# Up-projection of a hybrid encoder step: the A22 T4 product of two sets by seven inner products, its operands streamed from DRAM

## The chip, the cores and the metric

The kernel runs on one core of a Trainium2 chip. The metric is the device time of one execution in microseconds. Three runs of the kernel before gave 1512.61, 1510.98 and 1512.71 us (median 1512.61).

## The reference, cut to what matters

One encoder layer on 1024 prompt and 32 sample tokens, all in fp32: an input projection with attention, short convolution and gates, an output projection, and then the MLP, in which the change lies:

```
x = x + merged @ w_o
f = jnp.square(jax.nn.relu(rmsnorm(x, g_ffn) @ w_up)) @ w_down    # w_up 1024 x 4096
x = x + f
```

The row factor of rmsnorm is applied after w_down (its square, `rs2`), so the up-projection needs only x times g_ffn.

## The kernel before, in words

Tokens lie along the free dimension: T = 1056 columns, halves of 528 (`TH`) and quarters of 264 (`TQ`). Every fp32 product is three matmuls of a high and a low part (`h`, `l`): the high part is a cast on ScalarE, the low part a subtraction on VectorE. One "set" is 256 columns of w_up, so there are 16 sets; a set is a 2 x 2 matrix of weight blocks (A11 to A22, with four k-blocks of 128 each) times a 2 x 2 matrix of token blocks (B11 to B22). It is done by the seven products of Strassen's scheme in Winograd's form: A11 B11, A12 B21, S1 T1, S2 T2, S3 T3, S4 B22 and A22 T4, where S1 to S4 are sums of weight blocks and T1 to T4 sums of token blocks. One such outer product has, for each of two quarters, 4 k-blocks x 3 matmuls of 264 columns = 12 matmuls (L362 to L376).

Sets 0 and 1 run alone. From set 2 on, sets run in pairs (`seven_pair`, L480), seven pairs in all. In a pair the products A12 B21 of both sets are one product of a 2 x 2 matrix of weight blocks by a 2 x 2 matrix of token blocks, and that one again is done by seven inner products of 2 k-blocks x 3 = 6 matmuls each (`inner_product`, L348): 42 matmuls instead of 48. Its token sums (`inner_t`) stay in SBUF. The other twelve products of a pair are outer ones.

`manual_schedule` fixes the order on TensorE, ScalarE, VectorE and POOL as it is written. `run` (L617) advances the pair's body by one step (to the next `yield`) and then every generator in `side` by one step, so `after(n, g)` does the first piece of g behind the body's step n + 1. DMAs issued on SP are placed by the compiler. Side work: `prepare` (L217) splits the outer weights of a set (POOL sums, ScalarE casts, VectorE low parts), `prepare_inner` (L256) those of the joined product, `pair_loads` fetches weights, `mid_sums` (L1731) makes and stores the T1 to T4 of the hidden values after relu and square, `mean_squares` (L1702) makes `rs2`. Split outer weights live in four buffers (`SHB`), raw weights in four, large tiles (4224 bytes a partition, `blk`) in 37. PSUM groups come from a pool of four (`many`) and one of two (`few`), two more tiles belong to `tps`. In the last pair the first weights and hidden tiles of the down-projection are split as well (L2416 to L2420), and the down-projection's loop (L2432) splits the next step's weights one step ahead.

Of the kernel before, what the change touches and what calls it, by code (L numbers as in the profile page):

```python
# [15 lines left out]
P = 128  # L16
# [59 lines left out]
def tile_step(  # L76
# [81 lines left out]
    def group(name, n=TT, pool_=None):  # L158
        p_ = pool_ or pools[turn[0] % len(pools)]
        turn[0] += pool_ is None  # L160
        return p_.tile([P, TW], F32, tag="g", name=name)[:, :n]
# [24 lines left out]
        nc.scalar.copy(d[:, 0, :], src)  # L186
        dve(d[:, 1, :], src, d[:, 0, :].bitcast(F32), op=sub)

    def half_w(src, name):
        h, l = (wpool[0].tile([P, 4, P], F32R, tag=f"s{x}", name=f"s{x}{name}", bufs=SHB) for x in "hl")  # L190
        nc.scalar.copy(h, src)  # L191
        return (h, l), partial(dve, l, src, h.bitcast(F32), op=sub)

# [62 lines left out]
    def prepare_inner(key, odd):  # L256
# [38 lines left out]
        low()  # L295
        yield

    def inner_operands(name, g, load):
# [48 lines left out]

    def inner_product(name, w, b, p_=None, pool_=None):  # L348

        o = {"B11": low_t[0][0], "B21": low_t[1][0], "B22": low_t[1][1]}.get(b) or inner_t[b]  # L350
        new = p_ is None
        if new:
            p_ = group(f"ps_in{name}", TQ, pool_)
        on = dict(skip_group_check=not new)
        wh, wl = w
        for k in range(2):
            nc.tensor.matmul(p_, wh[:, k, :], o[:, 0, k, :], start=new and k == 0, stop=False, **on)
            nc.tensor.matmul(p_, wh[:, k, :], o[:, 1, k, :], start=False, stop=False, **on)
            nc.tensor.matmul(p_, wl[:, k, :], o[:, 0, k, :], start=False, stop=k == 1, **on)
        return p_  # L360
# [116 lines left out]
                done("near")  # L477
        done("21")

    def seven_pair(s0, s1, key, m, last, after=({}, {})):  # L480

        def tile_of(k, i):
            return wpool[0].tile([P, TQ], F32, tag=k, name=f"{k}_{s0}{i}")
# [42 lines left out]
        def sixth(i, t):  # L526
            product(i, "A22", "T4", t, x[i][t])
            last(m(i, 1), q[t][1], x[i][t])

        for f in (first, second, third, fourth):  # L530
            for t in range(2):
                f(0, t)
                yield
# [51 lines left out]
    def after(n, *gens):  # L585
        for _ in range(n):
            yield
        for g in gens:
            yield from g
# [18 lines left out]
    def pair_side(nm, a, b, then=None):  # L608

        order = ("S1", "A11", "S2", "S3", "S4", "A22")  # L610
        side.append(after(3, prepare(f"{nm}{b}", (4, 6, 8, 10, 13, 15), (f"{nm}{a}e", f"{nm}{a}o", 1), order)))
# [179 lines left out]
    def md(k, s_):  # L791
# [8 lines left out]
    cvd = dpool.tile([4, 2, P, T], F32, name="cvd")  # L800
    ed = dpool.tile([KD, P, T], F32, name="ed")
    edt = dpool.tile([P, 2, 2 * P], F32, name="edt")
    inner_s = {
        (k, p): {a: dpool.tile([P, NP_, P], F32, name=f"di{k}{p}{a}") for a in ("S1", "S2", "S3", "S4")}
        for k in NESTED for p in range(2)
# [851 lines left out]
    def wo_unit(n):  # L1657
# [41 lines left out]

        return load, body  # L1700

    def mean_squares():  # L1702
# [12 lines left out]

# [28 lines left out]
        dve(tb[:, 0, :], m2[:, a], ta[:, 1, :], op=sub)  # L1744
        nc.sync.dma_start(md("T4", s_), tb[:, 0, :])

    def up_hooks(i, s_, m):
# [24 lines left out]

        def c21():
            side.append(later_(partial(done, 1, 0, "B21")))

        return {"11": c11, "22": c22, "12": c12, "near": near, "21": c21}

# [4 lines left out]
    def up_pair(a, b):  # L1782
        ms = {}

        def m(i, j):
            if (i, j) not in ms:
                ms[i, j] = blk(f"m{j + 1}_{(a, b)[i]}")
            return ms[i, j]

        return seven_pair(  # L1790
            f"u{a}", f"u{b}", f"u{a}y", m, relu2, [up_hooks(i, (a, b)[i], partial(m, i)) for i in range(2)]
        )

    def up_source(a, b):
# [592 lines left out]
    with tc.manual_schedule(engines=MM):  # L2387
        def all_t():
            o, e = x1[-1], x1[-2]
            raw_t[KD // 2 - 1] = sums(KD // 2 - 1, e, o)  # L2390
            yield
            for n, parts in enumerate(LATE_T):
                for k, j in parts:
                    part_raw(f"T{k}", j)
                if n == 2:
                    for j in range(3):
                        fetch_t(j, 1)
                yield

        side += [all_t(), first_w.pop(), after(2, prepare("u1", at=(9, 11, 13, 15, 17, 19)))]  # L2400
# [10 lines left out]
        run(up_set(1))  # L2411
        for a in range(2, NSET, 2):
            more = a + 2 < NSET
            pair_side("u", a, a + 1, up_source(a + 2, a + 3) if more else None)
            if not more:
                side.append(after(13, call(fetch_upto, 2), call(sum_w, 0), call(sum_w, 1)))  # L2416
                side.append(after(15, *(call(fetch_mid, "P1", 0, j) for j in range(4))))
                side.append(after(18, call(high_w, 0), call(high_mid, "P1", 0, 0), call(low_w, 0), call(low_mid, "P1", 0, 0)))
                side.append(after(20, *(call(f, "P1", 0, j) for j in (1, 2) for f in (high_mid, low_mid))))
                side.append(after(23, call(high_mid, "P1", 0, 3), call(low_mid, "P1", 0, 3), call(fetch_mid, "P1", 1, 0), call(fetch_mid, "P1", 1, 1)))  # L2420
            run(up_pair(a, a + 1))
        while side:
            run(range(1))
# [152 lines left out]
```

## Time and profile before

| what | value |
|---|---|
| median of three runs | 1512.61 us |
| profiled execution | 1510.11 us |
| its span, first to last instruction | 1508.4 us |
| granted TensorE clock, mean | 0.999 |
| TensorE busy | 1495.6 us |
| VectorE / ScalarE / POOL busy | 1149.1 / 794.6 / 377.7 us |

A busy TensorE only says that a matmul was under way: matmuls overlap, a duration of 0.28 us stands beside a spacing of 0.12 us between starts. Idle time of another engine costs nothing by itself.

### The profile page before, as it was taken

Reading aid. Unit: us, or ns where it says so; the run is one execution under the profiler, and the core shown is the slowest. Engines: PE = TensorE matmul, PEld = TensorE weight load, DVE = VectorE, ACT = ScalarE, POOL = GpSimd, SP = SyncE. Lnnn points to the kernel's source line nnn. Section 1 sums busy time; section 2 is a strip of 40 time slices with the busy share of each in tenths; the row PEclk is TensorE's granted clock in tenths of the full one; section 3 lists DMA queues with packets and bytes.
Section 4 is the critical chain, followed back from the end, with each engine's and each line's share of the span. In section 5 each row is a group of like instructions: output and inputs, shape, how many; then the busy total and the mean of one; then the engine's idle time right before and its main releaser. Section 6 shows DMA issues by size and latency. Waiting matters only on the chain.

```text
span 1508.4 us, 29451 instructions
## 1 busy us (share of the span) xinstructions
PE 1495.6 (99%) x11556; PEld 1481.3 (98%) x11556; DVE 1149.1 (76%) x1628; ACT 794.6 (53%) x1575; POOL 377.7 (25%) x330
## 2 busy tenths in 40 slices
PE   9999999999999999999999999999999999999997
PEld 9999999999999999999999999999999999999997
DVE  6867788879578989876786676666688878879766
ACT  7654444445467767433475555555655433334655
POOL 0434334444121222003324333332000000000251
PEclk9999999999999999999999999999999999999999
DMA  6624425423688766655644434444979767855443
GB/s 242 213 74 171 169 57 198 156 84 98 226 265 251 199 157 154 221 181 184 230 151 146 148 129 144 157 157 150 322 280 284 245 192 238 289 185 166 142 129 123
DMA packets 117259, 275.52 MB, mean 183 GB/s; under 512 B 14048, under 2 KB 31072, under 8 KB 117120
## 3 DMA queue, kind: packets, MB, share of 16 engines
q1 hardware_dynamic: 112144, 259.39, 50.9%
q0 software_dynamic: 1728, 6.29, 2.5%
q10 hardware_dynamic: 3248, 7.96, 1.6%
q8 instruction: 91, 1.49, 0.4%
q14 instruction: 48, 0.39, 0.1%
HBM read 196.10 MB, written 85.88 MB: 187 GB/s over the span
## 4 chain that ended last, share of the span: by engine, by line
PE 93%; DVE 4%; issue 1%; ACT 1%; DMA 1%; ACTq 0%; DVEq 0%; SPq 0%
PE ps_dn L2016 6%; PE ps_dn L2015 6%; PE ps_dn L2014 6%; PE ps_A11i L374 5%; PE ps_A11i L373 5%; PE ps_A11i L375 5%; PE ps_A11u L374 4%; PE ps_A11u L373 4%; PE ps_A11u L375 4%; PE av L1294 2%; PE ps_S1i L375 2%; PE ps_S1i L374 2%; PE ps_S1i L373 2%; PE ps_wo L135 2%; PE ps_wo L133 2%; PE ps_wo L134 2%
## 5 line engine op out<-in xcount | busy, mean ns | idle before, releaser
L2016 PE MATMUL ps_dn<-fhP,wlo_dn 128*128 128x264 f32 x768 | 218.9, 285 | 0.0
L2015 PE MATMUL ps_dn<-flP,whi_dn 128*128 128x264 f32 x768 | 218.7, 285 | 0.1
L2014 PE MATMUL ps_dn<-fhP,whi_dn 128*128 128x264 f32 x768 | 218.2, 284 | 0.0
L2015 PEld LDWEIGHTS ps_dn<-flP,whi_dn 128*128 128x128 f32 x768 | 144.4, 188 | 0.4 <-DVE flP L1880 0.4
L2016 PEld LDWEIGHTS ps_dn<-fhP,wlo_dn 128*128 128x128 f32 x768 | 144.6, 188 | 0.2 <-DVE wlo_dn L1864 0.2
L2014 PEld LDWEIGHTS ps_dn<-fhP,whi_dn 128*128 128x128 f32 x768 | 144.6, 188 | 0.0
L1239 DVE TENSOR_TENSOR_SCAN r<-r 128x128 f32<-128x128 f32 (+3 forms) x64 | 86.8, 1356 | 5.3 <-POOL r L1232 5.3
L2229 POOL TENSOR_TENSOR xx<-xx,pgs 128x400 f32<-128x400 f32 (+1 forms) x17 | 20.0, 1183 | 281.1 <-DVE pgs L2228 281.1
L373 PE MATMUL ps_A11i<-T,shS_i 128*128 128x264 f32 x288 | 82.4, 286 | 0.0
L374 PE MATMUL ps_A11i<-T,shS_i 128*128 128x264 f32 x288 | 82.2, 285 | 0.0
L375 PE MATMUL ps_A11i<-T,slS_i 128*128 128x264 f32 x288 | 81.9, 284 | 0.0
L373 PE MATMUL ps_A11u<-T,shS_u 128*128 128x264 f32 x256 | 73.3, 286 | 0.0
L374 PE MATMUL ps_A11u<-T,shS_u 128*128 128x264 f32 x256 | 72.9, 285 | 0.0
L375 PE MATMUL ps_A11u<-T,slS_u 128*128 128x264 f32 x256 | 72.8, 284 | 0.0
L1232 POOL TENSOR_SCALAR_AFFINE_SELECT r<-r 128x128 f32<-128x128 f32 x64 | 35.9, 562 | 131.9 <-ACT r L1225 131.8
L1858 ACT CAST whi_dn<-raw_dn 128x1024 fp32r<-128x1024 f32 x31 | 32.6, 1052 | 66.9 <-PE ps_dn L2015 54.7
L1880 DVE TENSOR_TENSOR flP<-mrP,fhP 128x1056 fp32r<-128x1056 f32 x48 | 59.9, 1252 | 6.2 <-ACT fhP L1875 6.2
L135 PE MATMUL ps_wo<-mh,wlo_wo 128*128 128x352 f32 x192 | 62.0, 323 | 0.0
L134 PE MATMUL ps_wo<-ml,whi_wo 128*128 128x352 f32 x192 | 61.9, 322 | 0.0
L133 PE MATMUL ps_wo<-mh,whi_wo 128*128 128x352 f32 x192 | 61.6, 323 | 0.0
L251 DVE TENSOR_TENSOR slS_i<-s_i,shS_i 128x512 fp32r<-128x512 f32 x54 | 48.2, 892 | 13.1 <-ACT shS_i L191 12.8
L1279 DVE TENSOR_TENSOR at<-pa,at 128x512 fp32r<-128x512 f32 (+2 forms) x96 | 50.4, 548 | 9.3 <-ACT at L1278 8.4
(1711 smaller groups left out, 5789.0 us busy)
## 6 DMA issues: line engine op xcount, KB each, us to landing
raw_dn<-in_w_down_dram SPq DMA_DIRECT2D x59, 512.0 KB, 5.3
mrP<-mdT SPq DMA_DIRECT2D x32, 528.0 KB, 6.1
mdB<-m SPq DMA_DIRECT2D x48, 264.0 KB, 2.1
mrP<-mdB SPq DMA_DIRECT2D x24, 528.0 KB, 6.7
s<-gd SPq DMA_DIRECT2D x16, 528.0 KB, 5.4
mdT<-ta SPq DMA_DIRECT2D x32, 264.0 KB, 2.9
raw_pg<-in_w_ple_gate_dram SPq DMA_DIRECT2D x15, 512.0 KB, 3.5
gd<-m_i SPq DMA_DIRECT2D x12, 528.0 KB, 2.9
```

Of the source, the lines that this page charges most:

```text
L133: nc.tensor.matmul(ps, wh, xh[k][:, cols], start=(k == order[0]), stop=False)
L134: nc.tensor.matmul(ps, wh, xl[k][:, cols], start=False, stop=False)
L135: nc.tensor.matmul(ps, wl, xh[k][:, cols], start=False, stop=(k == order[-1]))
L373: nc.tensor.matmul(p_, wh[:, k, :], h, start=new and n == 0, stop=False, **on)
L374: nc.tensor.matmul(p_, wh[:, k, :], l, start=False, stop=False, **on)
L375: nc.tensor.matmul(p_, wl[:, k, :], h, start=False, stop=z, **on)
L1239: nc.vector.tensor_tensor_scan(rev, rev, rev, 1.0, ALU.mult, ALU.bypass)
L1279: nc.vector.tensor_tensor(al, pt[:, :nb, :], ah.bitcast(F32), op=ALU.subtract)
L1880: dve(l, mraw.pop(v), opd[v].bitcast(F32), op=sub)
L2014: nc.tensor.matmul(ps, hi[:, j, :], oh, start=j == 0, stop=False)
L2015: nc.tensor.matmul(ps, hi[:, j, :], ol, start=False, stop=False)
L2016: nc.tensor.matmul(ps, lo[:, j, :], oh, start=False, stop=j == NP_ - 1)
```

## The change

From the pair of sets 4 and 5 on (`both = a > 2`), the products A22 T4 of the two sets are also one product done by seven inner products. Its weight parts are made in the pair itself (`prepare_last`; the outer A22 splits go). Its token operands are made once, in the pair of sets 2 and 3 (`last_operands`), stored to DRAM (`zd`, seven tiles), and each pair loads each of them again shortly before its use (`z_load`). The order inside a pair is rewritten (`seven_both`): the inner results are accumulated on the PSUM groups of the outer ones and folded in from SBUF (`fold`), and the relu of that quarter block comes afterwards, over both quarters (hook `c21`). Moved with it: the split order of a pair's second set, the weight fetches, the start of the next set's splits (step 13 instead of 14), the `near` hook, the eight reciprocals (now two in each of the pairs 6 to 12), and the splits for the down-projection at the end.

```diff
+    def prepare_last(key, a, b):
+        ra, rb = (raws[f"{x}r"][:, 4:8, :] for x in (a, b))
+        w = ws[key] = {}
+        def pair_of(src, name, kinds):
+            d = blk(f"{name}{key}", F32R, [P, 2, 4, P])
+            nc.scalar.copy(d[:, 0], src)
...
+            return partial(dve, d[:, 1], src, d[:, 0].bitcast(F32), op=sub)
+        yield
+        yield
+        low = pair_of(ra, "lw", ("A11", "A12"))
+        yield
+        low()
+        yield
+        t = wpool[0].tile([P, 4, P], F32, tag="s", name=f"ls{key}", bufs=4)
+        a11, a12, a21, a22 = ra[:, 0:2, :], ra[:, 2:4, :], rb[:, 0:2, :], rb[:, 2:4, :]
+        dve(t[:, 0:2, :], a21, a22, op=add)
+        dve(t[:, 2:4, :], a11, a21, op=sub)
+        yield
+        dve(a11, t[:, 0:2, :], a11, op=sub)
+        low = pair_of(t, "lx", ("S1", "S3"))
+        yield
+        dve(a12, a12, a11, op=sub)
+        low()
+        yield
+        yield
+        low = pair_of(ra, "ly", ("S2", "S4"))
+        yield
+        low()
+        for _ in range(8):
+            yield
+        w["A22"], low = half_w(rb[:, 2:4, :], f"a{key}", 2)
+        yield
+        low()
+    def last_operands(nm, load):
+        for b, j0, f in (("B11", 0, 0), ("B21", 2, 0), ("B22", 2, 1), ("B12", 0, 1)):
+            if b in zd[nm]:
+                for j in range(2):
+                    nc.sync.dma_start(zd[nm][b][:, :, j, :], oper["T4"][j0 + j][:, :, quarters[f]].bitcast(F32))
...
+                for i, o in lows:
+                    nc.scalar.copy(d[:, i, 0, :], x[o])
+                yield
+                for i, o in lows:
+                    dve(d[:, i, 1, :], x[o], d[:, i, 0, :].bitcast(F32), op=sub)
+                    nc.sync.dma_start(zd[nm][kinds[i]][:, :, k, :], d[:, i].bitcast(F32))
+    def z_load(nm, b):
+        zt[b] = t = blk(f"zt{b}", F32R, [P, 2, 2, TQ])
+        nc.sync.dma_start(t.bitcast(F32), zd[nm][b])
...
+        def outer(a, b, on=None, pool_=few):
+            return inner_product(f"l{a}{key}", ws[f"{key}l"][a], zt.pop(b), on, pool_)
+        def fold(i, t, by):
+            dve(m(i, 1)[:, q[t][1]], x[i][t], by, op=add)
...
-        return after(n, prepare(f"{nm}{a}", (6, 8, 10, 11, 14, 16), (e, o, 0))), after(n + 3, prepare_inner(f"{nm}{a}y", o))
+        return after(n, prepare(f"{nm}{a}", (6, 8, 10, 11, 14, 16)[: 6 - both], (e, o, 0))), after(n + 3 + (n > 12), prepare_inner(f"{nm}{a}y", o))
...
+        at = (5, 6, 10, 13, 15) if both else (4, 6, 8, 10, 13, 15)
+        if both:
+            order = ("S1", "A11", "S2", "S4", "S3")
+            side.insert(0, prepare_last(f"{nm}{a}yl", f"{nm}{a}", f"{nm}{b}"))
-            for n, f in zip((6, 8, 10, 19), pair_loads(nm, *then)):
+            for n, f in zip((10, 9, 11, 20) if both else (6, 8, 10, 19), pair_loads(nm, *then)):
-            side.extend(ahead_of(nm, then[1], 14))
+            side.extend(ahead_of(nm, then[1], 14 - bool(both), more))
...
-            nc.vector.reciprocal(rs2[:, i : i + 132], rs2[:, i : i + 132])
-            yield
+            turned_over.append(partial(nc.vector.reciprocal, rs2[:, i : i + 132], rs2[:, i : i + 132]))
...
-                side.append(after(2, mid_sums(s_, m(0), m(1))))
+                side.append(after(2 + both, mid_sums(s_, m(0), m(1))))
...
+                elif n == 7:
+                    nc.scalar.dma_start(td[3][KD // 2 - 1], raw_t[KD // 2 - 1]["T4"])
+            if a == 2:
+                side.append(after(1, last_operands("u", lambda to, j: nc.sync.dma_start(to, td[3][j]))))
+                side.append(after(16, call(high_w, 0), call(high_mid, "P1", 0, 0), call(low_w, 0), call(low_mid, "P1", 0, 0)))
+                side.append(after(19, *(call(f, "P1", 0, j) for j in (1, 2) for f in (high_mid, low_mid))))
+                side.append(after(21, call(high_mid, "P1", 0, 3), call(low_mid, "P1", 0, 3), call(fetch_mid, "P1", 1, 0), call(fetch_mid, "P1", 1, 1)))
+                side.append(after(23, call(high_w, 1), call(low_w, 1)))
+            if 4 < a < 14:
+                side.extend(after(n, call(lambda: turned_over.pop()())) for n in (16, 20))
```

The three lines of the last pair stood at 18, 20 and 23, and the fourth is new; in the down-projection's loop the first step no longer splits the second weight. The order of `seven_both` by steps ("/" is the end of a step; `outer` is an inner product of the new seven, `inner` one of A12 B21):

```
1 to 4:  first(0,0) / first(0,1) / z_load B11, second(0,0) / second(0,1) /
5 to 7:  z_load T1, third(0,0) / third(0,1) / fourth(0,0) /
8:   xl = outer A11 B11 (tps); p4 = copy xl; fourth(0,1) /
9:   z_load T2; xi = inner A11 B11; p1[0] += xi; fifth(0,0) /
10:  z_load B21; zl = outer S1 T1 (few); s4 = copy zl; fifth(0,1) /
11:  zi = inner S1 T1 (few); i5 = copy zi; inner S2 T2 on xi; p1[1] += xi /
12:  outer S2 T2 on xl; v4 = xl - s4; c11 = inner A12 B21 (many); m(0,0) = c11 + p1[0] /
13:  z_load B22; inner S3 T3 on xi; c[1] = xi - i5; outer A12 B21 on x[0][0]; fold(0,0,p4) /
14:  z_load T3; second(1,0) /
15:  inner S4 B22 on zi; m(0,0) = p1[1] - zi; first(1,1) /
16:  inner A22 T4 on xi; c[0] = copy xi; outer S4 B22 on x[0][1]; fold(0,1,v4) /
17:  z_load T4; first(1,0) /   18:  second(1,1) (few) /
19:  outer S3 T3 on xl; v4 = xl - s4; u4 = copy xl; third(1,1) /
20 to 23:  third(1,0) / fifth(1,1) / fourth(1,0) / fifth(1,0) /
24:  fourth(1,1); outer A22 T4 on x[1][0]; fold(1,1,v4); fold(1,0,u4) /
```

In `fourth` VectorE reads the PSUM group x, in `fifth` z; in `first` and `third` ScalarE (for set 1's `first`: VectorE) reads x, in `second` ScalarE reads z.

## Rows read from the trace of the kernel before

**Rows 1.** The page: span, and busy time of each engine.
```profile
span 1508.4 us, 29451 instructions
...
PE 1495.6 (99%) x11556; PEld 1481.3 (98%) x11556; DVE 1149.1 (76%) x1628; ACT 794.6 (53%) x1575; POOL 377.7 (25%) x330
```
**Rows 2.** The page: granted TensorE clock in 40 slices, in tenths.
```profile
PEclk9999999999999999999999999999999999999999
```
**Rows 3.** Waits of TensorE in the whole span: total us, times, longest.
```profile
PE ps_idle L1409 <- DVE eps_t L104: 1.1, 1, 1.1
...
PE av L1294 <- ACT o1h L1311: 0.2, 1, 0.2
```
**Rows 4.** Timeline of TensorE: first matmuls of two neighbouring pairs (start us, us).
```profile
951.94 0.28 PE L373 MATMUL ps_A11u<-B,shA_u 128*128 128x264 f32 x1
...
992.21 0.28 PE L373 MATMUL ps_A11u<-B,shA_u 128*128 128x264 f32 x1
```
**Rows 5.** Windows: one pair, and a stretch with eight reciprocals (busy us, clock, DMA).
```profile
870.50:907.00 36.50, 36.50 (x294) 35.86 (x293) 30.43 (x43) 19.18 (x41) 15.79 (x12) 1.00 0.37 133
...
952.00:992.30 40.30, 40.30 (x332) 40.30 (x332) 24.19 (x37) 21.98 (x47) 15.35 (x12) 1.00 0.42 147
```
**Rows 6.** Timeline of VectorE in the pair from 951.94 us.
```profile
951.85 0.68 DVE L251 TENSOR_TENSOR slS_u<-raw_u10r,shS_u 128x512 fp32r<-128x512 f32 x1
...
955.39 1.80 DVE L1735 TENSOR_TENSOR ta<-m 128x528 f32<-128x528 f32 x1
957.23 1.68 DVE L1738 TENSOR_TENSOR m<-m,m 128x528 f32<-128x528 f32 x1
...
966.02 0.43 DVE L524 TENSOR_TENSOR m<-u_u,ps_S1u 128x264 f32<-128x264 f32 x1 [1.03 <-PE ps_S1u L375]
...
984.28 0.69 DVE L1735 TENSOR_TENSOR ta<-m 128x528 f32<-128x528 f32 x1
...
986.05 1.24 DVE L1738 TENSOR_TENSOR m<-m,m 128x528 f32<-128x528 f32 x1
...
991.76 0.71 DVE L1744 TENSOR_TENSOR tb<-m,ta 128x528 f32<-128x528 f32 x1 [2.57 <-DMA mdT<-m]
```
**Rows 7.** Timeline of POOL in the same pair.
```profile
955.00 1.62 POOL L253 TENSOR_TENSOR raw_u11r<-raw_u11r 128x512 f32<-128x512 f32 x1
...
984.50 1.08 POOL L281 TENSOR_TENSOR raw_u12o<-si_u12y,raw_u12o 128x256 f32<-128x256 f32 x1 [0.70 <-DVE wlo_u12y L276]
```
**Rows 8.** Timeline of ScalarE in the same pair.
```profile
980.66 0.38 ACT L511 COPY s_u<-ps_S1u 128x264 f32<-128x264 f32 x1 [2.00 <-PE ps_S1u L375]
980.94 0.62 ACT L191 CAST shS_u<-s_u 128x512 fp32r<-128x512 f32 x1
981.46 0.65 ACT L1729 ACTIVATE m<-m 128x528 f32<-128x528 f32 x1
...
985.17 0.41 ACT L267 CAST whi_u12y<-raw_u12o 128x256 fp32r<-128x256 f32 x1
...
990.94 0.39 ACT L1726 ACTIVATE m<-ps_A11u 128x264 f32<-128x264 f32 x1 [2.63 <-PE ps_A11u L375]
```
**Rows 9.** DMA issues from 750 to 1075 us: count, KB each, median us to landing.
```profile
mrP<-mdB SPq DMA_DIRECT2D x6, 528.0 KB, 6.1
...
raw_u12r<-in_w_up_dram SPq DMA_DIRECT2D x1, 512.0 KB, 4.0
```
**Rows 10.** Source line of the reciprocals: ns min/median/max, first and last start us.
```profile
L1713 DVE RECIPROCAL ssq<-ssq x8: 920/966/968, 888.8 to 900.8; 128x132 f32<-128x132 f32 x8
```
**Rows 11.** Timeline of TensorE at the start of the down-projection.
```profile
1074.95 0.28 PE L2014 MATMUL ps_dn<-fhP,whi_dn 128*128 128x264 f32 x1
1075.38 0.39 PE L2015 MATMUL ps_dn<-flP,whi_dn 128*128 128x264 f32 x1
...
1079.13 0.28 PE L2015 MATMUL ps_dn<-flP,whi_dn 128*128 128x264 f32 x1
1079.43 0.39 PE L2016 MATMUL ps_dn<-fhP,wlo_dn 128*128 128x264 f32 x1
```

More of the change, by code (lines that the diff above doesn't have):

```diff
@@ L187, in part_t, with half_w @@
         dve(d[:, 1, :], src, d[:, 0, :].bitcast(F32), op=sub)
-    def half_w(src, name):
-        h, l = (wpool[0].tile([P, 4, P], F32R, tag=f"s{x}", name=f"s{x}{name}", bufs=SHB) for x in "hl")
+    def half_w(src, name, n=4):
+        h, l = (wpool[0].tile([P, 4, P], F32R, tag=f"s{x}", name=f"s{x}{name}", bufs=SHB)[:, :n, :] for x in "hl")
         nc.scalar.copy(h, src)
@@ new lines, in last_operands, with fetch_raw @@
+    def last_operands(nm, load):
[3 more added lines that the diff above has]
+                    nc.sync.dma_start(zd[nm][b][:, :, j, :], oper["T4"][j0 + j][:, :, quarters[f]].bitcast(F32))
+        raws_ = []
+        def fetch_raw(k):
+            raws_.append(blk(f"rl{nm}{k}", F32, [P, 2, TH]))
+            for i in range(2):
+                load(raws_[k][:, i, :], k + 2 * i)
+        fetch_raw(0)
+        for _ in range(3):
+            yield
+        for k in range(2):
+            raw = raws_[k]
+            x = [raw[:, i, j * TQ : j * TQ + TQ] for i in range(2) for j in range(2)]
+            for kinds in (("T3", "T1"), ("T2", "T4")):
+                d = blk(f"z{kinds[0]}{nm}{k}", F32R, [P, 2, 2, TQ])
+                lows = []
+                for i, kind in enumerate(kinds):
+                    o, a, b, op = {"T3": (3, 3, 1, sub), "T1": (1, 0, 1, sub), "T2": (0, 0, 3, add), "T4": (2, 2, 0, sub)}[kind]
+                    dve(x[o], x[a], x[b], op=op)
+                    lows.append((i, o))
+                if k == 0 and kinds[0] == "T2":
+                    fetch_raw(1)
+                yield
+                for i, o in lows:
+                    nc.scalar.copy(d[:, i, 0, :], x[o])
+                yield
+                for i, o in lows:
+                    dve(d[:, i, 1, :], x[o], d[:, i, 0, :].bitcast(F32), op=sub)
+                    nc.sync.dma_start(zd[nm][kinds[i]][:, :, k, :], d[:, i].bitcast(F32))
@@ L348, in inner_product @@
     def inner_product(name, w, b, p_=None, pool_=None):
-        o = {"B11": low_t[0][0], "B21": low_t[1][0], "B22": low_t[1][1]}.get(b) or inner_t[b]
+        o = b
+        if isinstance(b, str):
+            o = {"B11": low_t[0][0], "B21": low_t[1][0], "B22": low_t[1][1]}.get(b) or inner_t[b]
         new = p_ is None
         if new:
-            p_ = group(f"ps_in{name}", TQ, pool_)
+            p_ = group(f"ps_in{name}", TQ, pool_) if pool_ is not tps else tps.tile([P, 512], F32, tag="tp", name=f"ps_in{name}")[:, :TQ]
         on = dict(skip_group_check=not new)
@@ L478, in seven_late, with seven_pair @@
         done("21")
-    def seven_pair(s0, s1, key, m, last, after=({}, {})):
+    def seven_pair(s0, s1, key, m, last, after=({}, {}), both=None, more=None):
         def tile_of(k, i):
@@ L528, in sixth, with seven_both @@
             last(m(i, 1), q[t][1], x[i][t])
+        def outer(a, b, on=None, pool_=few):
+            return inner_product(f"l{a}{key}", ws[f"{key}l"][a], zt.pop(b), on, pool_)
+        def fold(i, t, by):
+            dve(m(i, 1)[:, q[t][1]], x[i][t], by, op=add)
+        def seven_both():
+            for f in (first, second):
+                for t in range(2):
+                    f(0, t)
+                    yield
+                    if f is first and t == 1:
+                        z_load(both, "B11")
+            third(0, 0)
+            yield
+            z_load(both, "T1")
+            third(0, 1)
+            yield
+            fourth(0, 0)
+            yield
+            tmp = blk(f"tmp{key}", F32, [P, 4, TQ])
+            p4, s4, u4 = (tmp[:, i, :] for i in range(3))
+            v4 = wpool[0].tile([P, TQ], F32, tag="v4", name=f"v4{key}", bufs=1)
+            xl = outer("A11", "B11", pool_=tps)
+            nc.scalar.copy(p4, xl)
+            fourth(0, 1)
+            yield
+            z_load(both, "T2")
+            done(0, "22")
+            xi = inner("A11", "B11")
+            dve(p1[0], xi, p1[0], op=add)
+            fifth(0, 0)
+            yield
+            z_load(both, "B21")
+            zl = outer("S1", "T1")
+            nc.scalar.copy(s4, zl)
+            fifth(0, 1)
+            done(0, "12")
+            yield
+            zi = inner("S1", "T1")
+            i5 = tile_of("s5", 2)
+            nc.scalar.copy(i5, zi)
+            inner("S2", "T2", xi)
+            dve(p1[1], xi, p1[1], op=add)
+            yield
+            outer("S2", "T2", xl)
+            dve(v4, xl, s4, op=sub)
+            c11 = inner("A12", "B21", pool_=many)
+            dve(m(0, 0)[:, q[0][1]], c11, p1[0], op=add)
+            yield
+            z_load(both, "B22")
+            c[1] = tile_of("p1", 2)
+            inner("S3", "T3", xi)
+            dve(c[1], xi, i5, op=sub)
+            outer("A12", "B21", x[0][0])
+            fold(0, 0, p4)
+            yield
+            z_load(both, "T3")
+            second(1, 0)
+            yield
+            inner("S4", "B22", zi)
+            dve(m(0, 0)[:, q[1][1]], p1[1], zi, op=sub)
+            done(0, "11")
+            first(1, 1)
+            yield
+            c[0] = tile_of("p1", 3)
+            inner("A22", "T4", xi)
+            nc.scalar.copy(c[0], xi)
+            outer("S4", "B22", x[0][1])
+            fold(0, 1, v4)
+            yield
+            z_load(both, "T4")
+            done(0, "21")
+            first(1, 0)
+            done(1, "11")
+            yield
+            second(1, 1, few)
+            yield
+            outer("S3", "T3", xl)
+            dve(v4, xl, s4, op=sub)
+            nc.scalar.copy(u4, xl)
+            third(1, 1)
+            yield
+            third(1, 0)
+            yield
+            fifth(1, 1)
+            yield
+            fourth(1, 0)
+            yield
+            fifth(1, 0)
+            done(1, "12")
+            done(1, "near")
+            yield
+            fourth(1, 1)
+            outer("A22", "T4", x[1][0])
+            fold(1, 1, v4)
+            fold(1, 0, u4)
+            done(1, "22")
+            done(1, "21")
+            yield
+            for k in (s0, s1, key, f"{key}l"):
+                ws.pop(k)
@@ L530, in seven_pair @@
+        if both:
+            yield from seven_both()
+            return
         for f in (first, second, third, fourth):
@@ L802, in tile_step @@
     edt = dpool.tile([P, 2, 2 * P], F32, name="edt")
+    zd = {
+        nm: {k: dpool.tile([P, 2, 2, TQ], F32, name=f"zd{nm}{k}") for k in ("B11", "B21", "B22", "T1", "T2", "T3", "T4")}
+        for nm in ("u",)
+    }
     inner_s = {
@@ L1745, in mid_sums, with up_hooks @@
         nc.sync.dma_start(md("T4", s_), tb[:, 0, :])
-    def up_hooks(i, s_, m):
+    def up_hooks(i, s_, m, both=False):
         def later_(*fs):
@@ L1770, in near @@
             if i:
-                side.append(after(2, mid_sums(s_, m(0), m(1))))
+                side.append(after(2 + both, mid_sums(s_, m(0), m(1))))
         def c21():
-            side.append(later_(partial(done, 1, 0, "B21")))
+            fs = (partial(done, 1, 0, "B21"),)
+            side.append(later_(*((partial(relu2, m(1), halves[0]),) if both else ()), *fs))
         return {"11": c11, "22": c22, "12": c12, "near": near, "21": c21}
@@ L1788, in m @@
             return ms[i, j]
+        both = a > 2
         return seven_pair(
-            f"u{a}", f"u{b}", f"u{a}y", m, relu2, [up_hooks(i, (a, b)[i], partial(m, i)) for i in range(2)]
+            f"u{a}", f"u{b}", f"u{a}y", m, relu2, [up_hooks(i, (a, b)[i], partial(m, i), both) for i in range(2)],
+            "u" if both else None, "u" if a + 2 < NSET else None,
         )
```

20 lines of the change are left out of this document (12 added, 8 removed).

## The prediction

> **What bounds the kernel now.** The page's engine line comes first: TensorE is busy for 1495.6 us of a span of 1508.4 us, the slices show no gap and full clock throughout, and the list of what TensorE waited for has ten entries, from 1.1 us down to 0.2, under 6 us together [rows 1 to 3]. So the time is the number of matmuls times their spacing, and an edit counts by the matmuls that it removes and by the waits of TensorE that it makes. In the stretch that changes, the first matmuls of two neighbouring pairs start at 951.94 and 992.21 us [rows 4]: 40.27 us. A pair has 330 matmuls of 264 columns (twelve outer products of 24, and 42 for the joined A12 B21 product), so the spacing is 40.27/330 = 0.1220 us, with no gap. VectorE is busy 24.2 us and ScalarE 22.0 us of that pair [rows 5], so both have room; a second row shows VectorE at 30.4 of 36.5 us, while TensorE never stops.
>
> **What the change takes away.** A22 T4 of both sets is 48 matmuls; seven inner products of 6 are 42. It applies to the pairs from set 4 on, six of the seven. 6 x 6 = 36 matmuls x 0.1220 us = 4.39 us, all of it on TensorE's path.
>
> **What it adds, per pair.** VectorE: three splits of 512 columns instead of two (+0.68), one of 256 and four sums of 256, priced like a sum of 264 at 0.43 (2.15), four folds and two v4 from PSUM (2.58) [rows 6]: +5.4 us, and in sets 6 to 12 two reciprocals of 0.97 us [rows 10]: 24.2 becomes 29.6 or 31.5 of 39.5 us. ScalarE: one more cast of 512 (0.62), one of 256 (0.41), three copies (1.14), and two whole relus of 0.65 in place of four of 0.39 from PSUM (-0.26) [rows 8]: +1.9, so 23.9 of 39.5 us. No row shows a fold; it lies between the sum of a PSUM group and an SBUF tile of its size (0.43) and a split of twice the size (0.68), and I take the first, which has its very operands. These cost nothing while TensorE's next reads and overwrites are met, so I set the new order against TensorE's clock. One step of 12 matmuls is 1.46 us, one of 18 is 2.20 us; steps 8, 9, 10, 15, 19 and 24 have 18. From a pair's start, steps 7, 10, 13, 17, 20 and 24 end at 10.3, 16.9, 21.3, 27.9, 33.0 and 39.5 us. Five places are near:
>
> (a) Step 7 overwrites the PSUM group whose copy ScalarE makes after step 5. The S1 split of the coming set takes the buffer of S4, so it waits for step 23 of the pair before (37.4 us of it). Behind it come three casts and a relu until 1.0 us of the new pair, the first copy (1.9), a cast of S3, a square and two relus (4.1), a copy, two squares and a copy (5.7), the lw cast (6.3), a copy that waits for 6.0 us (6.5), two casts (7.6) and then the copy in question: 7.9, needed at 8.8. I took 0.52 for an operation of 0.62 and so on, since starts back to back lie 0.1 us closer than the durations [rows 8].
> (b) Step 11 takes the third of two spare PSUM groups, so the copy of S1 T1 must be out: 15.4 + 0.15 + 0.38 = 15.9, needed at 16.9.
> (c) Inner S3 in step 13 overwrites what VectorE reads after step 11. Before it stand a sum at 17.0 and two splits of 0.68, so the read ends at 19.2; it is needed at 19.8. In before this gap was 30 matmuls (3.7 us), now it is 12.
> (d) The streamed B21 block is fetched in step 10, at 14.7 us at the latest, and read from 20.5 us. 528 KB against a 512 KB weight block's 4.0 us and the 528 KB mrP's 6.1 us [rows 9]: it lands at 18.7 to 20.8. I take the weight's, since the traffic around it is the same. The other six blocks have 5.9 to 13 us.
> (e) The read of the fourth product of set 1 after step 22. VectorE's queue: sum and reciprocal from 27.9 (1.40), split 0.68; v4 waits for 30.2; 0.43 + 0.43 + 0.69 + 0.69 + 0.68 + 0.69 gives 33.8; a wait for step 21 until 34.6; 0.43 + 0.68 + 0.97 + 0.69 + 0.43 gives 37.8. The last six matmuls of step 24 overwrite that group at 38.8.
>
> All five are met, by 0.6 to 1.9 us (at its far end (d) is missed by 0.3). Because the margins are so small I keep 0.8 us for small waits (six pairs, 0.13 each).
>
> **The other edits.** The T4 tiles free four of the 37 large buffers; one pair uses lw, lx, ly, tmp and up to three streamed blocks, at most nine beside the 28 fixed ones by my count. In before there were five, and VectorE waited 2.57 us for a store to free one, in step 22, without TensorE noticing (the row at 991.76) [rows 6]. Gone, that wait would be a gain for VectorE only. The pair of sets 2 and 3 also makes the operands: 8 sums and 8 splits of 264 on VectorE (16 x 0.43 = 6.9 us), 8 copies on ScalarE (3.0 us), four loads and 14 stores of 264 KB on SP. It keeps the old order with slack of 3.7 us or more at its reads; I cost it at nothing, and at 1 us if a buffer is late. SP, which works in order, gets 42 more loads of 528 KB (22 MB, and 3.7 MB per pair of 39.5 us is 94 GB/s on top of 147 [rows 5]). The one store issued on ScalarE's queue stands in set 0, where its data has long been ready: nothing. The weight fetches moved by 1 to 4 steps (the second block waits for the ly split) land by some 23.5 us, and POOL's sums of the next set start some 2 us later: their splits are due from step 20 on, 10 us off. The near hook waits a step longer, because its list is a step shorter: no shift. The reciprocals only change place; the three sums ahead of them share two PSUM tiles with the new l-sum, which leaves them one, and each is read two steps before the next: nothing. At the start of the down-projection TensorE now waits for the low halves: matmuls start 0.43 and 0.30 us apart instead of 0.12 [rows 11], 0.49 us too much. The splits come one to three steps earlier, the second weight's before the loop; I count these 0.5 us as gone (0 if the splits are late with VectorE's queue). Next in line there is the fourth low half, some 2 us behind the first matmul and read later still.
>
> Sum: 1510.11 (profiled) - 4.39 - 0.5 + 0.8 = 1506.0 us; the same -4.1 from the median of 1512.61 gives **1508.5 us**, on which I settle since what is measured is a median.
>
> **Rivals.** R1, the vector queue becomes the bound in steps 19 to 24. VectorE's sums of two SBUF tiles took 1.80 and 1.68 us beside POOL's 1.6 us operations; later in the same pair, beside POOL's 1.08 us ones, 0.69 and 1.24 [rows 6, 7]. Five POOL operations fall into (e)'s queue, since the second half of them now waits for the late S3 split. It decides once the lengthening passes 1.8 us (0.8 of waiting before 34.6, 1.0 of slack). If four of the five cost 1.11 (1.80 - 0.69) each, TensorE waits 4.4 - 1.8 = 2.6 us in each of the five pairs that prepare a next one: 1508.5 + 13 = 1521 us, slower. Against it: the two later rows, 0.55 more in all beside the very operations that fall into the queue, and no wait at 30.4 of 36.5 us.
> The Trainium skill (SBUF — State Buffer, "Who interferes with whom") says that a VectorE instruction with two SBUF inputs and a GpSimd instruction that reads SBUF exclude each other for a whole instruction, whichever started first. By it all five could cost, 5.5 - 1.8 = 3.7 us a pair and 1527 us; the trace agrees at 955.39 (1.80) and not at 984.28 (0.69).
> R2, the streams are late. At 6.1 us and an issue 0.3 later, (d) misses by 0.6 us in six pairs: 3.5 us given back, 1512.0. For it: the added 94 GB/s and mrP's 6.1. Against: the weight's 4.0, and that SP may issue earlier.
> R3, the ScalarE copy of (a) is late by two more 0.65 operations: 0.4 us x 5 pairs = 2.0, 1510.5. For it: the S1 split's wait puts everything behind 37.5 us. Against: 0.9 us of slack.
> R4, the change doesn't do what it says: fewer matmuls with wider spacing. At 40.27/324 = 0.1243 us all 4.4 are given back: 1512.9. Against it: the 42 inner matmuls of the same 264 columns that a pair already has lie inside the 40.27 us.
>
> **Chances.** 0.2% of 1512.61 is 3.0 us, about what a measurement of this kernel tells from nothing. Forecast 0.58 (faster 0.54, its upper edge within 0.2% 0.04; its own range 1506.9 to 1510.2), R1 0.12 (slower 0.11, same 0.01), R2 0.17 (same 0.15, slower 0.02), R3 0.10 (faster 0.02, same 0.08), R4 or anything else 0.03 (faster 0.02, slower 0.01). Together faster 0.58, same 0.28, slower 0.14. The range is 1506.9 to 1514.0: low end 4.39 + 0.5 gained without small waits (1507.7) less 0.8, half the spread of the three runs, high end R2 and R3 together (1508.5 + 3.5 + 2.0); R1 is left out.
>
> **What would show it.** 36 matmuls fewer; pair pitch 39.5 us from set 4 on (40.27 means all was given back); no TensorE wait on the m or p_u sums (R1, c), on the streamed zt blocks (R2), or on ScalarE's u_u copy (R3); no wider spacing than 0.13 us in the first down-projection step. The forecast is wrong if the pitch of the pairs 6 to 12 stays over 39.9 us.

## The result: slower by 5.8 us, and the profile after

The changed kernel takes 1517.26 us (median of six runs, 1515.28 to 1519.9), the kernel before 1511.46 (six runs, 1510.98 to 1512.71): ratio 1.0037, interval 1.0024 to 1.0050. The forecast was 1508.5, faster. The profiled execution took 1518.27 us.

The page of the changed kernel shows the matmuls that were to go (36 fewer), and a longer span:

```profile
span 1515.8 us, 29647 instructions
...
PE 1495.2 (99%) x11520; PEld 1479.0 (98%) x11520; DVE 1195.8 (79%) x1716; ACT 805.4 (53%) x1601; POOL 386.9 (26%) x330
```

So TensorE lost time while it had less to do. The waits of TensorE of the whole span (engine, line, releaser: total us, times, longest), against [rows 3]:

```profile
PE ps_inA12u2y L439 <- DVE m L606: 3.7, 1, 3.7
PE ps_f L1237 <- DMA raw_i<-in_w_in_dram: 1.6, 2, 1.3
PE ps_A11i L455 <- ACT u_i L598: 1.3, 2, 0.7
PE ps_idle L1606 <- DVE eps_t L104: 1.1, 1, 1.1
...
PE ps_inlS1u10y L439 <- DMA ztT<-zduT: 0.4, 1, 0.4
PE ps_A11i L457 <- DVE slA_i L251: 0.3, 1, 0.3
```

New are the first, which is in the pair of sets 2 and 3, the third and the last, which are in the input projection (with two of 0.3 and 0.2 us that are left out here), and the one on a streamed block. The wait on ps_f at the very start depends on when the first weights land: up to 2.5 us in the profiles of this study, 0.4 and 1.2 in the kernel before without and with the edit of e2.

To see where the time lies, the span is cut at the first matmul of each stage, read from TensorE's timeline. Profiled executions, us:

| stretch | before | after | difference |
|---|---|---|---|
| start to first ps_A11i | 55.01 | 55.87 | +0.86 |
| ps_A11i to first ps_A11u (input projection to up-projection) | 693.02 | 696.60 | +3.58 |
| ps_A11u to first ps_dn (up-projection) | 324.73 | 328.40 | +3.67 |
| ps_dn to first ps_pg (down-projection) | 323.83 | 322.70 | -1.13 |
| rest, with 1.7 and 2.5 us outside the span | 113.52 | 114.70 | +1.18 |

The first row changes from one execution to the next (54.9 to 57.6 us in the profiles of this study). The last was 113.5 us in both profiles of the kernel before, without and with the edit of e2, and 113.9 to 114.8 in all others; why was not traced.

**The pairs reach the forecast pitch where nothing waits.** The same matmul of two neighbouring pairs (start us, duration us), against [rows 4]:

```profile
1018.26 0.28 PE L439 MATMUL ps_inS1u12y<-yiT1m,whi_u12y 128*128 128x264 f32 x1
...
1057.79 0.28 PE L439 MATMUL ps_inS1u14y<-yiT1m,whi_u14y 128*128 128x264 f32 x1
```

That is 39.53 us instead of 40.27. From set 6 on the distances between these marks (the pitch of a pair) are 39.82, 40.20, 39.52 and 39.53 us; the 40.20 holds the wait on the streamed block. The windows of the changed kernel (stretch, its length, busy us of PE, PEld, DVE, ACT, POOL, then clock and DMA) have a stretch of a pair's length in their last row, most of it in sets 12 and 13, and ahead of it the place where the time went:

```profile
785.00:825.00 40.00, 36.25 (x275) 35.83 (x274) 33.31 (x61) 21.88 (x51) 15.43 (x11) 0.91 0.54 182
...
811.90:815.90 4.00, 0.29 (x3) 0.08 (x1) 0.45 (x2) 1.24 (x3) 0.00 (x0) 0.83 0.96 349
815.90:821.40 5.50, 5.47 (x25) 5.47 (x26) 5.40 (x14) 3.80 (x10) 0.00 (x0) 0.50 0.47 156
...
1003.10:1042.60 39.50, 39.50 (x326) 39.50 (x325) 32.99 (x54) 23.03 (x49) 16.64 (x12) 1.00 0.71 246
```

**The pair of sets 2 and 3.** From inner S1 of this pair to that of the next, 48.47 us pass. Before it was 40.28, and 12 outer matmuls more now lie between these two marks (12 x 0.122 = 1.46), so 41.74 would be even: 6.7 us are lost. TensorE's timeline, the two marks and what lies between them:

```profile
808.83 0.28 PE L439 MATMUL ps_inS1u2y<-yiT1m,whi_u2y 128*128 128x264 f32 x1
...
811.91 0.28 PE L457 MATMUL ps_A11u<-T,slA_u 128*128 128x264 f32 x1
815.93 0.59 PE L439 MATMUL ps_inA12u2y<-B,whi_u2y 128*128 128x264 f32 x1 [3.74 <-DVE m L606]
816.32 0.42 PE L440 MATMUL ps_inA12u2y<-B,whi_u2y 128*128 128x264 f32 x1
...
821.16 0.39 PE L441 MATMUL ps_inA11u2y<-yiT3m,wlo_u2y 128*128 128x264 f32 x1
821.38 0.29 PE L455 MATMUL ps_S1u<-T,shS_u 128*128 128x264 f32 x1
...
857.30 0.28 PE L439 MATMUL ps_inS1u4y<-yiT1m,whi_u4y 128*128 128x264 f32 x1
```

4.02 us lie between two starts that should be 0.12 apart (3.90 lost), and the next 24 matmuls take 5.45 us instead of 2.93 (2.52 lost), since they run 0.22 apart at a granted clock of 0.50, the lower of the two levels. VectorE, ScalarE and the DMA queue on SyncE show why; a number in brackets is idle time before the instruction, and what ended it:

```profile
800.89 1.69 DVE L1942 TENSOR_TENSOR tb<-m,ta 128x528 f32<-128x528 f32 x1
802.50 2.96 DVE L360 TENSOR_TENSOR rlu<-rlu 128x264 f32<-128x264 f32 x2
...
809.25 0.42 DVE L724 TENSOR_TENSOR p_u<-ps_inA11u2y,p_u 128x264 f32<-128x264 f32 x1
815.45 0.43 DVE L606 TENSOR_TENSOR m<-u_u,ps_S1u 128x264 f32<-128x264 f32 x1 [5.78 <-DMA zduT<-zT3u]
```
```profile
812.54 0.72 ACT L366 CAST zT2u<-rlu 128x264 fp32r<-128x264 f32 x2 [6.11 <-DMA mdT<-tb]
```
```profile
806.63 0.33 SPq L115 DMA_DIRECT2D raw_u4r<-in_w_up_dram  x1
...
807.53 0.38 SPq L1943 DMA_DIRECT2D mdT<-tb  x1
...
809.73 1.19 SPq L370 DMA_DIRECT2D zduT<-zT3u  x2
811.78 0.83 SPq L2619 DMA_DIRECT2D rlu<-td  x2
```

The first write to m1 of set 2 needs a large buffer and gets it when the store of the made T3 and T1 operands has landed. That operation is also the one that frees the PSUM group which the inner A12 product is waiting for. ScalarE stands for a large buffer too, until the store of an older sum (tb of set 1) lands.

SyncE came late to that store. Its wait there, in the list from 796 to 815 us:

```profile
SPq L115 <- POOL s_u L253: 6.3, 1, 6.3
```

VectorE had made tb by 802.58 us, but SyncE stood for 6.3 us, until 806.63, at the load of a weight block that waits for GpSimd, and issued the store of tb at 807.53. (The kernel before has such a hold of 6.8 us, and no wait of TensorE.) Two of the sums for the operands were slow as well: 2.96 us at 802.50, while GpSimd made sums too, where the next two took 0.89. How much of the stall comes from either was not tested.

### The profile page after: what moved, and what is told of

It is laid out like the page before. It is cut to its first block, busy times and chain, and to the rows that moved or that the text cites. A ratio compares the mean times of both kernels' runs of the same rounds, so it can differ in the third digit from the quotient of the medians.

```text
span 1515.8 us, 29647 instructions
## 1 busy us (share of the span) xinstructions
PE 1495.2 (99%) x11520; PEld 1479.0 (98%) x11520; DVE 1195.8 (79%) x1716; ACT 805.4 (53%) x1601; POOL 386.9 (26%) x330
## 4 chain that ended last, share of the span: by engine, by line
PE 87%; DVE 6%; ACT 3%; DMA 2%; issue 2%; SPq 0%; ACTq 0%; DVEq 0%
PE ps_dn L2215 6%; PE ps_dn L2217 6%; PE ps_dn L2216 6%; PE ps_A11i L457 4%; PE ps_A11i L455 4%; PE ps_A11i L456 4%; PE ps_A11u L455 3%; PE ps_A11u L456 3%; PE ps_A11u L457 3%; PE av L1491 2%; PE ps_wo L134 2%; PE ps_wo L135 2%; PE ps_wo L133 2%; PE ps_S1i L457 2%; PE ps_S1i L456 2%; PE ps_S1i L455 2%
## 5 line engine op out<-in xcount | busy, mean ns | idle before, releaser
L251 DVE TENSOR_TENSOR slS_i<-s_i,shS_i 128x512 fp32r<-128x512 f32 x54 | 53.3, 987 | 15.3 <-ACT shS_i L191 15.3
```

Source lines behind the costliest of these rows:

```text
L251: lows.pop()()
```

## The experiments

All times are medians, the ratio against runs of the kernel before on the same chip (medians of 1511.3 to 1511.9). Differences between two edited kernels are differences of medians that partly come from different chips.

**The input projection.** Its pairs use ahead_of too, so they got the later preparation.

```
e1: after(n + 3 + (n > 12 and nm == "u"), prepare_inner(...))    # changed kernel
e2: after(n + 3 + (n > 12 and nm == "i"), prepare_inner(...))    # kernel before
```

> The changed kernel with the preparation of a pair's inner weights put back one step earlier in the input projection only (ahead_of delays it by n + 3 + 1 for the up-projection alone). Theory A: the shared helper cost the input projection time: six TensorE waits of 0.3 to 0.95 us (3.4 us together) that the trace of before does not have; they vanish, the first copy of the up-projection starts 3.4 us earlier, and the time is about 1513.9 against 1517.3. Rival B: those waits are variation of this stage or come from something else: 1516.5 to 1518, the waits stay.

> The kernel before with that one edit alone: in the input projection the preparation of the inner weights starts one step later. Theory A: 2.5 to 3.5 us slower than before, about 1514.5, with waits of the input projection's products on u copies and weight splits like those of the changed kernel. Rival B: the same as before within 0.5 us.

e1: 1514.75 (1.0024, 1.0015 to 1.0033), 2.5 us under the changed kernel. e2: 1514.06 (1.0017, 1.0008 to 1.0026), 2.6 us over the kernel before. The same stretch, input to up-projection, is 693.89 us in e1 and 696.13 in e2. The waits of TensorE from 60 to 425 us, e1 and then e2; the kernel before has none in this list:

```profile
PE ps_A11i L455 <- ACT u_i L598: 0.5, 1, 0.5
```
```profile
PE ps_A11i L373 <- ACT u_i L516: 1.3, 2, 0.7
PE ps_A11i L375 <- DVE slA_i L251: 0.3, 1, 0.3
```

Theory A holds: one step in a helper that another stage shares costs 2.5 us. The 0.87 us that e1 still has over before in this stretch lie at two places (0.70 us at the wait shown, 0.19 at 81.4 us); their cause was not traced, and they vary: the stretch took 693.1 to 695.4 us in the eight profiles with e1's edit.

**What making the operands costs at all.** e4 replaces the body of last_operands:

```
-  sums, ScalarE copies, splits, stores of zT* tiles (two raw and four made large buffers)
+  nc.sync.dma_start(zd[nm][kind][:, :, k, :], td[3][k + 2 * i].rearrange(...))
```

> The changed kernel with the sums, splits and large buffers of the made operands left out: in the same steps the T operands are copied unsummed and unsplit from DRAM to DRAM, so the seven products of step 8 get wrong T values. This prices all that making the operands costs in the pair of sets 2 and 3. Theory A: the stall and its half clock go, 6 to 6.6 us faster than the changed kernel, about 1511. Rival B: the stall comes from the other edits of that pair (the splits of the next pair sooner), not from the operands: less than 2 us faster.

e4: 1513.77 (1.0014, 1.0006 to 1.0023), 3.5 us under the changed kernel, between the two theories. Its profile has no wait in the pair of sets 2 and 3, whose pitch is 41.76 us, within 0.02 us of even; the stall is the operands'.

```profile
812.44 0.28 PE L418 MATMUL ps_inS1u2y<-yiT1m,whi_u2y 128*128 128x264 f32 x1
...
854.20 0.28 PE L418 MATMUL ps_inS1u4y<-yiT1m,whi_u4y 128*128 128x264 f32 x1
```

It lost 1.6 us in sets 0 and 1 instead, on copies by ScalarE that stood behind late loads there. Its runs spread over 6 us (1511.57 to 1517.65), which I can't attribute.

**Which part of the making.** All from here on have e1's edit, so they are compared with 1514.75, except e3.

```
e3: zip((10, 9, 11, 20) if nm == "u" else (6, 8, 10, 19), pair_loads(...))  # changed kernel
e6: -  if k == 0 and kinds[0] == "T2": fetch_raw(1)
    +  after the stores of k == 0: two steps, fetch_raw(1), three steps
e5: side.append(after(5, last_operands(...)))                              # was after(1, ...)
```

> The changed kernel with the loads of the next pair's weights moved from steps 6, 8, 10, 19 to 10, 9, 11, 20 in the pair of sets 2 and 3 too, so that SyncE no longer holds the stores of the made operands behind a load that waits for GpSimd. Theory A: the 5.8 us wait of VectorE for a large buffer comes from the late issue of the zT3 store; the 3.7 us TensorE stall and the 24 matmuls at half clock after it vanish: 5 to 6.5 us faster than the changed kernel, about 1511. Rival B: the buffers are short whatever the order of issue (the made operands and the m tiles exceed the pool): the stall stays at 2 us or more, 1514 to 1517.

> Base of this and the next three: the changed kernel with the early preparation back in the input projection (1514.75 median). In the pair of sets 2 and 3 the second pair of raw T tiles takes its large buffer only five steps later, after the first four stores. Theory A: the 37 large buffers are short by one or two for some 6 us, and the buffer that the second raw tile takes at 810 us is the one that m1 of set 2 waits for: VectorE's 5.8 us wait falls under 2.5 us, the TensorE stall under 1 us, no half clock, 3.5 to 6 us faster than the base: 1509 to 1511. Rival B: VectorE's wait is for a slot that only the T3 store frees, whoever asks: the stall stays above 3 us, 1514 to 1516. Rival C: the stall goes, but another of 1 to 3 us comes where the operands now finish late: about 1512.

> Base as above; making the operands starts at step 5 of the pair of sets 2 and 3 instead of step 1, past the m tiles and sums of set 1 that still hold buffers. Theory A (buffers short only where both overlap): the stall before m1 of set 2 goes, 5 us or more faster than the base: about 1509.5. Rival B (the pool is short all through the pair): the wait moves to m1 or m2 of set 3, with a TensorE stall of 2 us or more there: 1512 to 1516.

e3: 1519.02 (1.0047, 1.0034 to 1.0060), against 1517.26. SyncE issued the two stores 0.9 us sooner, but they took 6.1 and 6.2 us to land instead of 4.8 and 5.0; VectorE still got its buffer at 815.82, after a wait of 6.52 us, and TensorE stood for 4.5. Issuing these two stores that much sooner does not help. The theory of the order of issue is not settled by it, since the edit did not take the hold away: SyncE stood 6.4 us for GpSimd again, at the load of another weight block, and issued the store of tb at 807.16, 0.4 us sooner than in the changed kernel. No run puts the stores of the sums ahead of these loads. e6: 1518.32 (1.0045, 1.0033 to 1.0058). The first wait did fall, from 5.8 us to 2.8, and TensorE's from 3.7 to 0.8; but the operands now come late, and ScalarE, standing on a late sum and then on a buffer, has TensorE wait elsewhere. VectorE, and the waits of TensorE from 795 to 830 us:

```profile
810.70 0.43 DVE L610 TENSOR_TENSOR m<-u_u,ps_S1u 128x264 f32<-128x264 f32 x1 [2.81 <-DMA mdT<-tb]
...
819.27 0.90 DVE L360 TENSOR_TENSOR rlu<-rlu 128x264 f32<-128x264 f32 x2 [3.98 <-DMA rlu<-td]
```
```profile
PE ps_A11u L459 <- ACT u_u L602: 4.2, 1, 4.2
PE ps_inA12u2y L443 <- DVE m L610: 0.8, 1, 0.8
```

e5: 1520.76 (1.0068, 1.0054 to 1.0082). TensorE waits at three places of that pair, 5.4, 1.7 and 1.6 us. So rival C of e6, larger than I gave it, and rival B of e5 in kind, with the longest stall at the made operands and not at m1 or m2 of set 3: asking at another time moves the wait. Not all of e5's is a buffer's. Its 5.4 us stand behind ScalarE's 4.22 us for a large buffer, but the 1.6 us stand behind VectorE's 5.46 us for raw tiles whose load SyncE issued late: it stood 6.8 us for GpSimd at a weight load and then 1.6 for a buffer.

**Fewer buffers.** e9 makes the same operands in one large buffer less per pair of raw tiles:

```
- d = blk(...)  for (T3, T1) and again for (T2, T4): high and low halves of two kinds each
+ d = blk(f"zh{nm}{k}", F32R, [P, 4, TQ])              # four high halves
+ four sums; then per part: nc.scalar.copy(d[:, o, :], x[o]); store high;
+ dve(x[o].bitcast(F32R), x[o], d[:, o, :].bitcast(F32), op=sub); store low from x[o]
+ fetch_raw(1) after the stores of k == 0, then five steps
```

> Base: the changed kernel with the early preparation back in the input projection (1514.75). The made operands need one large buffer less per pair of raw tiles: the four sums come first, the four high halves share one large buffer, each low half is written over its own sum, high and low are stored apart (16 stores of 132 KB instead of 8 of 264 KB), and the second pair of raw tiles is asked for after the first has been made, with five steps before it is used. Theory A (the pair of sets 2 and 3 was short by one or two large buffers, and in-order engines stood on it; asking later alone only moved the wait): no TensorE gap over 0.5 us from 795 to 830 us, the pitch of that pair falls from 48.5 to 41.8 us, 6 us faster than the base: 1508 to 1509.5, faster than the kernel before. Rival B (it is the DVE, ScalarE or DMA time of making them, not the buffers): a stall of 2 us or more stays in that pair, 1511 to 1515.

e9: 1510.17 (0.9992, 0.9984 to 1.0001), 4.6 us under e1, and no TensorE wait from 795 to 830 us. The pitch is 42.90 us; the 1.2 us over an even pair are nine starts 0.19 to 0.31 us apart, too short for the list of waits. ScalarE's casts run without a wait for a buffer, and VectorE stands for one for 1.1 and 0.9 us, unnoticed by TensorE. That was two changes, footprint and order, so e13 gives back the buffer alone:

```
- d = blk(f"zh{nm}{k}", F32R, [P, 4, TQ])
+ ds = [blk(f"zh{nm}{k}{p}", F32R, [P, 4, TQ]) for p in range(2)]     # each half filled
```

> The kernel with the low halves written in place (1510.17) and one thing put back: the four high halves lie in two large buffers, half filled, instead of in one. Nothing else changes: same instructions, same stores, same order. Theory A (large buffers are what is short): waits of VectorE or ScalarE for a buffer of 2 us or more come back in the pair of sets 2 and 3, with a TensorE gap of 1 us or more there; 1 to 5 us slower, 1511.5 to 1515. Rival B (the new order of sums and stores, not the buffers, took the stall away): no gap over 0.5 us in that pair, 1510 within 1 us.

e13: 1512.52 (1.0000, 0.9991 to 1.0010), 2.35 us over e9, or 1.8 with each set against the kernel before on its own chip; the two intervals overlap, so the time alone is weak evidence. The stronger is the profile, of the slowest of the ten runs. Its pitch is 45.02 us. The marks of e9 and then of e13, and what VectorE waits for in e13:

```profile
805.59 0.28 PE L442 MATMUL ps_inS1u2y<-yiT1m,whi_u2y 128*128 128x264 f32 x1
...
848.49 0.29 PE L442 MATMUL ps_inS1u4y<-yiT1m,whi_u4y 128*128 128x264 f32 x1
```
```profile
807.34 0.28 PE L442 MATMUL ps_inS1u2y<-yiT1m,whi_u2y 128*128 128x264 f32 x1
...
852.36 0.29 PE L442 MATMUL ps_inS1u4y<-yiT1m,whi_u4y 128*128 128x264 f32 x1
```
```profile
811.02 0.43 DVE L609 TENSOR_TENSOR m<-u_u,ps_S1u 128x264 f32<-128x264 f32 x1 [2.85 <-DMA mdT<-tb]
```

The store of tb is the one that e6 waited for. The waits of TensorE from 795 to 835 us, the longer one behind ScalarE's 1.55 us for a store of high halves:

```profile
PE ps_A11u L458 <- ACT u_u L601: 1.7, 1, 1.7
PE ps_inA12u2y L442 <- DVE m L609: 0.8, 1, 0.8
```

The same instructions with one more large buffer held bring the waits back: theory A holds, and the shortage of buffers is a cause that acts by itself. The pitch falls from 48.67 us in e1 to 45.02 in e13 and 42.90 in e9, so in these profiles one buffer is worth 2.12 us of 5.77. That the other 3.65 come from the later second load and the longer spacing is argued, not shown.

**The streams.** e7 is e1 with the load of B21 one step earlier; e8 is e5 and e7 together; e12 is e9 with B21 one step and T1 two steps earlier.

```
e7, e8, e12:  z_load(both, "T2"); z_load(both, "B21")   # B21 was one step later
e12:          if f is second and t == 0: z_load(both, "T1")   # was after third(0, 0)
```

> Base as above, with the load of the B21 stream one step earlier in every pair from set 4 on, so that it goes ahead of the two raw loads of 256 KB on SyncE's queue (one more large buffer for one step). Theory A (the wait of 1.07 us of the A12 x B21 products in the profiled run is a late stream, and such waits come in one or two pairs of each execution): waits on ztB are gone; 1 us faster, about 1513.7, and the runs spread less. Rival B: the load then waits for a large buffer, or pushes the T2 stream or the raw loads: no gain or 0.5 to 2 us slower, with waits on ztT or on splits.

> The last two edits together. If each does what theory A says, the gains add: 1508 to 1509, 2.5 to 3.5 us faster than the kernel before. If the start at step 5 only moves the stall, 1512 to 1515.

> The kernel of the run before this one, with the B21 stream's load one step earlier and the T1 stream's load two steps earlier, so that they go ahead of the raw loads and of the stores of the sums, which wait for VectorE, on SyncE's queue. Theory A (one or two waits of 0.4 to 1.6 us on ztT or ztB in each execution are loads held up on SyncE): the waits on ztT and ztB go, 1 to 1.5 us faster than the run before, 1507 to 1508. Rival B: two loads that hold large buffers for longer make the m tiles wait: pitches of 40.5 us or more from set 4 on, slower than the run before.

e7: 1514.34 (1.0021, 1.0012 to 1.0031), like e1 within the spread. The waits on ztB are gone from its profile; instead there is one on T1, whose load stood on SyncE behind stores of sums that VectorE had not made yet:

```profile
PE ps_inlS1u10y L439 <- DMA ztT<-zduT: 1.6, 1, 1.6
```

e8: 1521.07 (1.0061, 1.0048 to 1.0074): e5's stalls again. e12: **1508.29** (0.9978, 0.9969 to 0.9987), 1.9 us under e9 and 3.0 under the kernel before, the fastest of all. Waits on ztB and ztT are gone. Waits of TensorE from 795 to 1075 us, e9 and then e12:

```profile
PE ps_A11u L442 <- DMA ztB<-zduB: 0.9, 2, 0.7
PE ps_inlS1u10y L442 <- DMA ztT<-zduT: 0.5, 1, 0.5
```
```profile
PE ps_inS1u10y L442 <- ACT tmpu10y L651: 0.8, 1, 0.8
PE ps_inA12u2y L442 <- DVE m L609: 0.2, 1, 0.2
```

The new wait of 0.8 us is a buffer's, rival B in kind: ScalarE stood 3.31 us at a cast of sets 10 and 11, ahead of that copy, until a store of tb landed.

Medians, from after down: 1517.3, minus 2.5 (input projection), minus 4.6 (order and buffers of one pair), minus 1.9 (streams) is 1508.3. That this lies beside the forecast of 1508.5 is luck: the kernel before is 1.15 us below the median that the forecast started from, and the gain is smaller.

## Why the prediction was wrong

**Right: the gain of the pairs.** 36 matmuls fewer, pitch 39.52 and 39.53 us in the two pairs without a loss, against 39.5, at unchanged spacing; R4 is out. VectorE was busy for 32.99 us of such a pair (I had 31.5) and ScalarE 23.03 (23.9), and TensorE waited for neither at (a), (b), (c) or (e); R1 and R3 are out (R1's slow sums do show in the pair of sets 2 and 3, at 802.50).

**Right in kind, smaller: (d) and R2.** Blocks do land late, but in at most three pairs of a profile and by 0.1 to 1.6 us (e13, e7), not 0.6 in all six. In the changed kernel it is one, and with the other small losses it is more than the 0.8 us that I kept: from inner S1 of set 4 to the down-projection there are 48 matmuls fewer (5.86 us; 12 of them now lie ahead of this mark) and the time is 4.48 us shorter, so 1.4 us were given back, 0.6 of them at that block. T1, to which I gave ample time, was hit as well, since a load in SyncE's order waits for what the stores ahead of it wait for; I had set the landing time against the need and had not asked when SyncE comes to the load.

**Too small: the start of the down-projection.** 0.5 us were counted, 1.1 came. Its first matmuls are now 0.12 apart, where [rows 11] had 0.43 and 0.30; the starts right behind those, 0.23 and 0.22 apart, bring it to 0.7. The remaining 0.4 was not traced.

```profile
1080.87 0.29 PE L2215 MATMUL ps_dn<-fhP,whi_dn 128*128 128x264 f32 x1
1080.99 0.29 PE L2216 MATMUL ps_dn<-flP,whi_dn 128*128 128x264 f32 x1
```

**Wrong: the pair of sets 2 and 3.** "It keeps the old order with slack of 3.7 us or more at its reads; I cost it at nothing, and at 1 us if a buffer is late." It cost 6.7 us in the profile; less 4.4 for the matmuls and with the 1.4 above, that is the 3.7 us by which the up-projection grew. The slack was that of TensorE's reads against VectorE's and ScalarE's work, as if only busy time could be late. I counted the large buffers for the pairs from set 4 on, nine beside the 28 fixed, and not for this one, where the old sums of set 1, the m tiles of set 2 and up to six tiles of the made operands meet. The row for it stood in my own evidence: VectorE's 2.57 us for a store to free a buffer, five in use [rows 6]. Its bound was a store's time to landing on a loaded DMA (4.9 us, median of the two T3 and T1 stores in the changed kernel) and the time that the store stands on SyncE before (5.0 us for tb), and not 1; and both VectorE and ScalarE work in order, so that a wait for a tile that nobody needs soon held the copies and sums that TensorE needed at once. The half clock after the gap was in no bound either. Nor was the wait for a buffer gone from set 4 on, as the count of nine had it: ScalarE stood 2.1 us for one in sets 10 and 11, unnoticed by TensorE.

**Wrong: a part that I did not cost.** I read ahead_of's new delay as one of the up-projection. The diff shows no stage, but the pairs of the input projection call the same function with n = 14; 2.5 us.

Two readings were off without consequence: the list of [rows 3] has nine entries, not ten, and the sum at 984.28 [rows 6] says little against R1, since it began 0.22 us ahead of GpSimd's operation (984.50, [rows 7]).

With the two wrong parts mended and the streams issued sooner, the gain is 3.0 us (2.0 to 4.7 by the interval) where 4.1 was forecast. In e12's profile the up-projection takes 322.26 us, 2.47 less than before, where 3.6 were forecast (4.39 - 0.8); 1.0 of the 1.1 that are missing lies in the pair of sets 2 and 3 (pitch 42.74 against 41.74).

## What to carry to other kernels

Count the buffers of a pool for the stretch in which the new work is done, not only for the one in which it pays, and price a shortage at a store's time to landing, with what holds its queue ahead of it, on every in-order engine that asks for a tile there. When a wait for a buffer can be moved but not removed by asking sooner or later, make the footprint smaller. For each edited helper list all its callers before costing it.

## What the runs showed of the hardware

TensorE's clock was granted in full through gaps of 1.6 and 1.7 us (e7 from 973.9, e13 from 825.0 us: 1.00 in the gap and after it), but it was at 0.50 to 0.69 over the 5.5 us behind gaps of 3.2 to 5.4 us (changed kernel, e1, e3, e5, e6, e7, e8); 0.50 is the lower of its two levels, 1.2 instead of 2.4 GHz. In the changed kernel that turned a wait of 3.7 us into a loss of 6.4. The windows of e13's gap of 1.7 us and behind it, and the one behind e5's gap of 5.4 us:

```profile
825.00:826.60 1.60, 0.00 (x0) 0.00 (x0) 1.60 (x3) 1.60 (x5) 0.97 (x2) 1.00 0.67 234
826.70:832.00 5.30, 5.30 (x44) 5.30 (x45) 4.16 (x8) 3.57 (x8) 2.08 (x4) 1.00 0.72 239
```
```profile
821.90:827.40 5.50, 5.50 (x25) 5.50 (x26) 3.88 (x8) 0.88 (x2) 1.35 (x1) 0.50 0.48 171
```
